# Output projection, operand sums and down projection of a retention/ConvFFN step: weights reused between column ranges, sums in place, loads spread

## The chip, the cores and the metric

The kernel runs on one core of a Trainium2 chip. The metric is the device time of one execution in microseconds (us), as the median of the runs shown. Engines are called TensorE (PE, its weight loads PEld), VectorE (DVE), ScalarE (ACT), GpSimd (POOL) and SyncE (SP, which here only issues DMAs).

## The reference

One layer, 1024 prompt frames and 64 sample frames of width 1024, all in float32. The part that the change touches:

```python
def _layer(x, c, pos0, r0, s0, conv0, ...):
    ...
    mix = jnp.concatenate([o_r, o_g], axis=-1).astype(dt)
    x = x + g1 * jnp.einsum('bte,ed->btd', mix, w_out)

    h2 = _rmsnorm(x, g_norm_ffn) * (1.0 + sc2) + sh2
    a, up = jnp.split(jnp.einsum('btd,df->btf', h2, w_ffn_in), 2, axis=-1)
    buf = jnp.concatenate([conv0.astype(a.dtype), a], axis=1)
    conv = conv_b + conv_w[0] * buf[:, 0:T]
    for j in range(1, CONV_W):
        conv = conv + conv_w[j] * buf[:, j:j + T]
    y = jax.nn.silu(conv) * up
    x = x + g2 * jnp.einsum('btf,fd->btd', y, w_ffn_out)
    return x, r_new.astype(r0.dtype), s_new.astype(s0.dtype), buf[:, T:]
```

Before it stand a first norm, an input projection and two recurrent mixers (retention and gated linear attention), behind it a last norm. D_FF is 2816, the convolution has width 3.

## The kernel before

Every float32 matmul is made of three on parts: `cut(hi, lo, src)` lets ACT round `src` into `hi`, VectorE subtracts it from `src` into `lo`, and TensorE sums hi x hi, lo x hi and hi x lo. The kernel is one long instruction order for each engine; small generators (`flow.start`, `flow.tick`) put side work between the steps of the main loops, and an engine works through its own order strictly.

**Output projection.** The 1088 columns (frames) go in three ranges, c = 0, 1, 2, of 384, 384 and 320; in each range the eight output blocks m of 128 rows run one after the other. For each step a weight unit of `w_out` (512 KB) is loaded, cut into `hi` (ACT) and `lo` (VectorE) by `take()`, multiplied into `dX` in PSUM, and freed by `release()`. The input `x`, transposed on TensorE, is added with the gain (`xt`, tile names `ab`, `hf`, `cv`), stored to `d_x2` in HBM, and its squares are summed in `sqs`. While range c runs, the second norm of range c-1 (`norm2`, scaling on VectorE, bias on ACT) is put between its steps.

**Up projection.** A Strassen-like scheme makes it of seven products of half size; `product(q, p)` multiplies weight sums by an operand `X[p]`. An operand is a cut of sums of the normed input (`operand`, `sums_b`), a weight sum is made by `need_in` and cut by `prep_in` (`prep_to` does so ahead). With the first products the norm of range 2 is finished: sums of squares by matmuls with ones, the reciprocal root `nr` on VectorE, a broadcast by matmul, then scaling.

**Down projection.** The same scheme; KF = 11 row blocks of 128. The steps run in the order M p=1 (11 steps), A p=2 (two halves u, six steps of two row blocks), A p=4 (the same), M p=6, A p=3 (u=0), M p=7, A p=3 (u=1), then p=5. For each step the weights come through `C1`, `C2` or the tile `rw` (4 buffers), `y` comes from HBM through `ry` (3 buffers) or `rb` (3 buffers, loaded from GpSimd's queue) into `ba`. `load_to` issues loads five steps ahead, `sum_out` makes weight sums three ahead, `prep_out` cuts three ahead, and `prep_b` cuts two `ba` pieces for each A step. In p=2 the sum `rw + C1` was made by VectorE, stored to HBM (`d_e`, from GpSimd's queue) and loaded again for p=3. `x3` (tile names `x_k_h`) is the residual, 16 loads of 256 KB from `d_x2`, into which `add_to` adds each finished PSUM tile (`mn`, `al`).

Of the kernel before, what the change touches and what calls it, by code (L numbers as in the profile page):

```python
# [12 lines left out]
F32 = mybir.dt.float32  # L13
# [180 lines left out]
def stream_step_kernel(  # L194
# [400 lines left out]
    for _ in range(NC3):  # L595
        for m in range(KD):
            plan(w_out[0, :, m * P:(m + 1) * P], KD, P)
# [781 lines left out]
    d_e = {}  # L1379
# [42 lines left out]
    def load_x(c, k2):  # L1422
        xt = ab_tile("ab0")[:, 0:768].rearrange("p (j d) -> p j d", j=3)
        cs = slice(k2 * 256, (k2 + 1) * 256)
# [11 lines left out]
    def operand(p, half_k, half_t, pool):  # L1436
        t = X[p] = pool.tile([P, 2, 4, HT], F32R, name=f"X{p}", bufs=1)
        for i in range(4):
            src = hf[4 * half_k + i][:, half_t * HT:half_t * HT + HT]
            cut(t[:, 0, i], t[:, 1, i], src)  # L1440
            yield 1.0

    def sums_b(which, a, b):

        for i in range(4):
            h11, h12 = hf[i][:, a:b], hf[i][:, HT + a:HT + b]
            h21, h22 = hf[4 + i][:, a:b], hf[4 + i][:, HT + a:HT + b]
            if which == 1:
                sub(h11, h12, h11)
# [7 lines left out]
    def norm2(c, sqs):  # L1457
# [11 lines left out]
        for k in range(KD):  # L1469
# [5 lines left out]
            if c < 2:  # L1475
                yield 1.2
        if c == 1:
            yield from operand(1, 0, 0, xap)
            yield from operand(2, 1, 0, xap)
# [84 lines left out]
    xr = [load_x(0, 0)]  # L1564
    for c in range(NC3):
# [4 lines left out]
        for m in range(KD):  # L1570
            (hi, lo), = take()
            ps = pair("dX")
            i = c * KD + m
            if i % 2 == 0 and i + 2 < NC3 * KD:
                xr.append(load_x((i + 2) // KD, (i + 2) % KD // 2))
            mm3(ps[:, 0, 0:w], [(hi[:, k, :], lo[:, k, :], mxs[c][k][0][:, 0:w],
                                 mxs[c][k][1][:, 0:w]) for k in (4, 5, 6, 7, 0, 1, 2, 3)])
            release()
            for j in range(3):
                tr(ps[:, 1, j * P:(j + 1) * P], xr[i // 2][:, j, (m % 2) * P:(m % 2 + 1) * P])  # L1580
# [6 lines left out]
            if m == 0:  # L1587
# [6 lines left out]
            if c == 2 and m == 5:  # L1594
# [7 lines left out]
            if c == 2 and m == 6:  # L1602
# [5 lines left out]
                                  .rearrange("j (f p) -> (j f) p", p=P))  # L1608
                prep_to(4)
                for n in range(1, 5):  # L1610
                    need_in(0, n)
# [190 lines left out]
    product(0, 1)  # L1802
    next(gen)
    turn_vectors()
# [6 lines left out]
    sums_b(1, edge, HT)  # L1811
# [128 lines left out]
    def load_out(n):  # L1940
        st = osteps[n]
        kind, p = st[:2]
        if kind == "M":
# [3 lines left out]
            elif p == 7:  # L1947
                rw[n] = ld_w(wrow(i, 0, 512, 512))
            t = ry[n] = ft("ry")
            nc.sync.dma_start(out=t, in_=d_y[i][:, YI[p]])  # L1950
        elif kind == "A":
            u, i, k = st[2:]
            if p == 2:
# [4 lines left out]
            elif p == 3:  # L1958
                t = rw[n] = ft("rw", (P, 2, 256))
                nc.sync.dma_start(out=t[:, 0:k], in_=d_e[u, i])  # L1960
# [6 lines left out]
    def sum_out(n):  # L1967
        st = osteps[n]
        kind, p = st[:2]
        if kind == "M" and p == 6:  # L1970
            w = rw[n] = ft("rw")
            sub(w, C2[:, st[2]], C1[:, st[2]])
# [379 lines left out]
```

## Time and profile before

| | |
|---|---|
| median of 3 runs | 1502.03 us (1501.88 to 1509.65) |
| profiled execution | 1507.18 us, span 1505.4 us |
| mean granted TensorE clock | 0.972 |
| busy, share of the span | PE 91%, DVE 72%, ACT 42%, POOL 21% |
| DMA | 164.31 MB, mean 109 GB/s |

The span is that of the profiled execution, on the chip's own clock from first to last instruction; its own time is 1.8 us longer. A share of busy time is a mean over stages: mixers up to about 618 us, output projection from there to about 734 us, up projection to about 1219 us, down projection to about 1490 us, and the last norm.

### The profile page before, as it was taken

What the parts mean: (1) busy time and instruction counts of PE and PEld (TensorE: products, weight loads), DVE (VectorE), ACT (ScalarE), POOL (GpSimd) and SP (SyncE); (2) the same over time, 40 slices, a digit from 0 to 9 for tenths busy, and PEclk for the clock granted to TensorE, in tenths of its full rate; (3) what the DMA queues carried; (4) which work ended last, traced back from release to release, by engine and by line L of the source; (5) the groups of instructions that cost most, each with busy time, mean ns of one, the idle gap of its engine ahead of it and who ended that gap; (6) DMA issues with size and microseconds to landing.
All of it is one profiled execution on the core that took longest, in us unless ns stands there. A gap on an engine that the chain in (4) does not pass through costs nothing.

```text
span 1505.4 us, 23828 instructions
## 1 busy us (share of the span) xinstructions
PE 1374.1 (91%) x9082; PEld 1275.0 (85%) x9082; DVE 1088.3 (72%) x2006; ACT 631.0 (42%) x1275; POOL 309.2 (21%) x416
## 2 busy tenths in 40 slices
PE   5899888989989998899779999999999998799996
PEld 3778777879979988898779999999999986688875
DVE  6647878966885788766887777777777755668775
ACT  5635434432333223555554344444444333334343
POOL 3335424414342432411000000000000011200010
PEclk9999999999999999999789999999999999899998
DMA  8420102123223223365113233222332269654522
GB/s 256 153 73 15 43 17 74 43 84 100 88 73 101 86 62 94 123 191 180 48 42 106 78 106 106 77 69 95 106 106 91 92 209 312 203 166 137 175 83 103
DMA packets 159226, 164.31 MB, mean 109 GB/s; under 512 B 9770, under 2 KB 127880, under 8 KB 159112
## 3 DMA queue, kind: packets, MB, share of 16 engines
q1 hardware_dynamic: 147655, 123.73, 26.6%
q0 software_dynamic: 11456, 39.07, 7.5%
q8 instruction: 71, 1.16, 0.3%
q14 instruction: 44, 0.35, 0.1%
HBM read 129.95 MB, written 32.81 MB: 108 GB/s over the span
## 4 chain that ended last, share of the span: by engine, by line
PE 57%; DVE 23%; issue 6%; ACT 5%; DMA 4%; POOL 1%; SPq 0%; DVEq 0%; ACTq 0%; POOLq 0%
PE dX L234 25%; PE mm L234 10%; PE dA L234 8%; PE al L234 4%; PE mn L234 3%; PE o L234 3%; DVE qbd L91 2%; DVE lo L91 2%; DVE att L91 2%; DVE acc L91 2%; ACT hi L91 1%; DVE X L91 1%; DMA rb<-d_y 1%; DVE ab L91 1%; PE sc L234 1%
## 5 line engine op out<-in xcount | busy, mean ns | idle before, releaser
L234 PE MATMUL dX<-X,lo 128*128 128x272 f32 x1344 | 182.1, 292 | 5.4 <-DVE ab L91 3.4
L234 PEld LDWEIGHTS dX<-X,lo 128*128 128x128 f32 x1344 | 175.8, 191 | 6.5 <-ACT cv L91 3.0
L234 PE MATMUL dX<-X,hi 128*128 128x272 f32 x1296 | 174.8, 291 | 4.9 <-DVE ab L91 2.7
L234 PEld LDWEIGHTS dX<-X,hi 128*128 128x128 f32 x1296 | 168.7, 191 | 5.7 <-issue 2.9
L234 PE MATMUL mm<-act_hi,hi 128*128 128x384 f32 (+1 forms) x480 | 170.1, 354 | 0.3 <-DVE mix L91 0.2
L234 PE MATMUL mm<-act_lo,hi 128*128 128x384 f32 (+1 forms) x480 | 158.1, 329 | 0.1
L234 PE MATMUL mm<-act_hi,lo 128*128 128x384 f32 (+1 forms) x480 | 157.8, 329 | 0.0
L91 ACT CAST hi<-raw 128x512 fp32r<-128x512 f32 (+1 forms) x122 | 97.3, 799 | 77.4 <-DVE raw L91 65.9
L234 PE MATMUL al<-ba,hi 128*128 128x512 f32 x396 | 102.7, 402 | 9.0 <-DVE x L91 9.0
L234 PE MATMUL mn<-lo,hi 128*128 128x512 f32 x396 | 96.5, 398 | 7.8 <-ACT lo L91 6.1
L234 PEld LDWEIGHTS mn<-lo,hi 128*128 128x128 f32 x396 | 74.3, 190 | 27.6 <-ACT lo L91 8.6
L234 PEld LDWEIGHTS al<-ba,hi 128*128 128x128 f32 x396 | 72.6, 192 | 24.4 <-DVE x L91 10.3
L234 PEld LDWEIGHTS mm<-act_hi,hi 128*128 128x128 f32 x480 | 91.5, 191 | 1.9 <-DVE mix L91 0.5
L234 PEld LDWEIGHTS mm<-act_lo,hi 128*128 128x128 f32 x480 | 91.3, 190 | 0.8 <-POOL act_lo L91 0.3
L91 DVE SCALAR_TENSOR_TENSOR cv<-ab,cw,cv 128x1088 f32<-128x1088 f32 x44 | 59.2, 1347 | 43.7 <-ACT cv L91 43.7
L234 PEld LDWEIGHTS mm<-act_hi,lo 128*128 128x128 f32 x480 | 90.8, 189 | 0.0
L234 PE MATMUL mm<-hi,act_hi 128*128 128x256 f32 x288 | 88.6, 308 | 0.2 <-ACT hi L91 0.2
L234 PE MATMUL mm<-lo,act_hi 128*128 128x256 f32 x288 | 82.8, 288 | 2.9 <-DVE lo L91 2.9
L234 PE MATMUL mm<-hi,act_lo 128*128 128x256 f32 x288 | 82.3, 286 | 0.0
L91 POOL TENSOR_TENSOR acc<-acc,prod 128x512 f32<-128x512 f32 x42 | 64.4, 1534 | 82.1 <-ACT prod L91 81.3
L234 PE MATMUL dX<-act_hi,hi 128*128 128x384 f32 (+1 forms) x192 | 67.1, 350 | 7.9 <-DVE ab L91 4.0
L91 DVE TENSOR_TENSOR lo<-raw,hi 128x1024 fp32r<-128x1024 f32 x49 | 63.7, 1302 | 13.6 <-ACT hi L91 13.5
(348 smaller groups left out, 3124.7 us busy)
## 6 DMA issues: line engine op xcount, KB each, us to landing
raw<-in_w_ffn_in_dram SPq DMA_DIRECT2D x44, 512.0 KB, 3.8
raw<-in_w_ada_dram SPq DMA_DIRECT2D x32, 512.0 KB, 4.0
raw<-in_w_in_dram SPq DMA_DIRECT2D x28, 512.0 KB, 3.8
raw<-in_w_out_dram SPq DMA_DIRECT2D x24, 512.0 KB, 3.7
d_y<-cv POOLq DMA_DIRECT2D x22, 512.0 KB, 5.1
rb<-d_y POOLq DMA_DIRECT2D x44, 256.0 KB, 3.7
rw<-in_w_ffn_out_dram SPq DMA_DIRECT2D x41, 256.0 KB, 2.7
wa<-in_w_ada_dram SPq DMA_DIRECT2D x16, 512.0 KB, 4.9
```

What stands on the lines that cost most here:

```text
L91: return call(*args, **kw)
L234: T.matmul(out, lhsT, rhs, start=start, stop=stop, skip_group_check=more)
```

## The change

- The weight units of `w_out` run in an order that turns from range to range (`M_ORDER`). The last three units of a range are not released and serve the first three steps of the next: 18 units instead of 24 are loaded and cut.
- `x` is loaded in 24 pieces of 128 columns, into tiles of its own (`xr`), instead of 12 of 256.
- The operands `X1` and `X2` are cut by column ranges, 384 columns behind the norm of range 0 and 160 behind that of range 1, instead of 544 columns behind the norm of range 1.
- The last four subtractions of `sums_b(1, ...)` run on GpSimd within the norm of range 2. The first weight sums are spread over the last steps, and `product(0, 1)` is made in two halves around the sum of the squares.
- In the down projection `C1` is overwritten by `C2 - C1` in p=6, and p=7 and p=3 load their weights again and subtract `C1`. The sums `rw + C1`, the tile `d_e`, its twelve stores and its loads are gone.
- The loads of `x3`, `x3s` and `gbc`, before at steps 2 to 6, are spread over the steps by `X3_AT`, and the loads of the first three blocks of `C1` move from step 1 to steps 12 to 14.
- `finish` has one more `yield`.

```diff
@@ -594,4 +594,6 @@
         pcol(c0)
-    for _ in range(NC3):
-        for m in range(KD):
+
+    M_ORDER = ((0, 1, 2, 3, 4, 5, 6, 7), (5, 6, 7, 4, 3, 2, 1, 0), (2, 1, 0, 3, 4, 5, 6, 7))
+    for c in range(NC3):
+        for m in M_ORDER[c][3 if c else 0:]:
             plan(w_out[0, :, m * P:(m + 1) * P], KD, P)
@@ -1378,3 +1380,2 @@
     d_y = [scr.tile([P, 7, 512], F32, name=f"d_y{i}") for i in range(KF)]
-    d_e = {}
     YI = {1: 0, 7: 1, 2: 2, 3: 3, 5: 4, 6: 5, 4: 6}
@@ -1421,5 +1422,7 @@
 
-    def load_x(c, k2):
-        xt = ab_tile("ab0")[:, 0:768].rearrange("p (j d) -> p j d", j=3)
-        cs = slice(k2 * 256, (k2 + 1) * 256)
+    def load_x(n):
+        c, m = divmod(n, KD)
+        m = M_ORDER[c][m]
+        xt = wo.tile([P, 3, P], F32, tag="xr", name="xr", bufs=4)
+        cs = slice(m * P, (m + 1) * P)
         nb = 3 if c < 2 else 2
@@ -1435,10 +1438,12 @@
 
-    def operand(p, half_k, half_t, pool):
-        t = X[p] = pool.tile([P, 2, 4, HT], F32R, name=f"X{p}", bufs=1)
+    def operand(p, half_k, half_t, pool, a=0, b=HT):
+        if p not in X:
+            X[p] = pool.tile([P, 2, 4, HT], F32R, name=f"X{p}", bufs=1)
+        t = X[p]
         for i in range(4):
-            src = hf[4 * half_k + i][:, half_t * HT:half_t * HT + HT]
-            cut(t[:, 0, i], t[:, 1, i], src)
-            yield 1.0
+            src = hf[4 * half_k + i][:, half_t * HT + a:half_t * HT + b]
+            cut(t[:, 0, i, a:b], t[:, 1, i, a:b], src)
+            yield 0.8
 
-    def sums_b(which, a, b):
+    def sums_b(which, a, b, eng=None):
 
@@ -1448,3 +1453,3 @@
             if which == 1:
-                sub(h11, h12, h11)
+                (eng or V).tensor_tensor(out=h11, in0=h12, in1=h11, op=ALU.subtract)
             elif which == 3:
@@ -1475,6 +1480,9 @@
             if c < 2:
-                yield 1.2
+                yield 1.0
+            elif k == 3:
+                sums_b(1, 2 * CW - HT, HT, G)
+        if c < 2:
+            yield from operand(1, 0, 0, xap, CW * c, (CW, HT)[c])
+            yield from operand(2, 1, 0, xap, CW * c, (CW, HT)[c])
         if c == 1:
-            yield from operand(1, 0, 0, xap)
-            yield from operand(2, 1, 0, xap)
             sums_b(1, 0, 2 * CW - HT)
@@ -1563,3 +1571,3 @@
     n2 = []
-    xr = [load_x(0, 0)]
+    xr = [load_x(0), load_x(1)]
     for c in range(NC3):
@@ -1569,13 +1577,15 @@
             G.memset(sqs[:, w:CW], 0.0)
-        for m in range(KD):
-            (hi, lo), = take()
+        for n, m in enumerate(M_ORDER[c]):
+            keep = c < 2 and n > 4
+            hi, lo = take(n - 4 if keep else 1)[-1]
             ps = pair("dX")
-            i = c * KD + m
-            if i % 2 == 0 and i + 2 < NC3 * KD:
-                xr.append(load_x((i + 2) // KD, (i + 2) % KD // 2))
+            i = c * KD + n
+            if i + 2 < NC3 * KD:
+                xr.append(load_x(i + 2))
             mm3(ps[:, 0, 0:w], [(hi[:, k, :], lo[:, k, :], mxs[c][k][0][:, 0:w],
                                  mxs[c][k][1][:, 0:w]) for k in (4, 5, 6, 7, 0, 1, 2, 3)])
-            release()
+            if not keep:
+                release()
             for j in range(3):
-                tr(ps[:, 1, j * P:(j + 1) * P], xr[i // 2][:, j, (m % 2) * P:(m % 2 + 1) * P])
+                tr(ps[:, 1, j * P:(j + 1) * P], xr[i][:, j, :])
             xt = hf[m][:, c * CW:c * CW + w]
@@ -1586,3 +1596,3 @@
             nc.gpsimd.dma_start(out=d_x2[:, m, c * CW:c * CW + w], in_=xt)
-            if m == 0:
+            if n == 0:
                 S.activation(out=sqs[:, 0:w], in_=xt, func=AF.Square)
@@ -1593,3 +1603,3 @@
             flow.tick()
-            if c == 2 and m == 5:
+            if c == 2 and n == 4:
                 do_lows(True)
@@ -1601,3 +1611,2 @@
                 raw_loads()
-            if c == 2 and m == 6:
                 ct = ab_tile("ab0")
@@ -1608,5 +1617,7 @@
                                   .rearrange("j (f p) -> (j f) p", p=P))
+            if c == 2 and n == 5:
+                prep_to(2)
+                need_in(0, 3)
+            if c == 2 and n == 6:
                 prep_to(4)
-                for n in range(1, 5):
-                    need_in(0, n)
         if c < 2:
@@ -1801,4 +1812,7 @@
     gen = norm2(2, sqs)
-    product(0, 1)
+    need_in(0, 2)
+    need_in(0, 4)
+    product(0, 1, 0, 2)
     next(gen)
+    product(0, 1, 2, 4)
     turn_vectors()
@@ -1810,3 +1824,2 @@
     product(1, 1)
-    sums_b(1, edge, HT)
     all_of(operand(5, 0, 0, xbp))
@@ -1947,3 +1960,3 @@
             elif p == 7:
-                rw[n] = ld_w(wrow(i, 0, 512, 512))
+                rw[n] = ld_w(wrow(i, 1, 512, 512))
             t = ry[n] = ft("ry")
@@ -1952,3 +1965,3 @@
             u, i, k = st[2:]
-            if p == 2:
+            if p in (2, 3):
                 rw[n] = ld_w(wpair(i, k, 1, u * 256), k)
@@ -1957,5 +1970,2 @@
                          ld_w(wpair(i, k, 0, 512 + u * 256), k))
-            elif p == 3:
-                t = rw[n] = ft("rw", (P, 2, 256))
-                nc.sync.dma_start(out=t[:, 0:k], in_=d_e[u, i])
 
@@ -1970,6 +1980,5 @@
         if kind == "M" and p == 6:
-            w = rw[n] = ft("rw")
-            sub(w, C2[:, st[2]], C1[:, st[2]])
+            sub(C1[:, st[2]], C2[:, st[2]], C1[:, st[2]])
         elif kind == "M" and p == 7:
-            sub(rw[n], C1[:, st[2]], rw[n])
+            sub(rw[n], rw[n], C1[:, st[2]])
         elif kind == "A" and p == 3:
@@ -1977,5 +1986,3 @@
             w = rw[n][:, 0:k]
-            sub(w, w, C2[:, i:i + k, u * 256:u * 256 + 256])
-
-    stores = []
+            sub(w, w, C1[:, i:i + k, u * 256:u * 256 + 256])
 
@@ -1987,3 +1994,3 @@
             c, y = main_slots(n)
-            w = C1[:, i] if p == 1 else rw.pop(n)
+            w = rw.pop(n) if p == 7 else C1[:, i]
             cut(c[:, 0], c[:, 1], w)
@@ -2006,6 +2013,2 @@
                 plus(C2[:, i:i + k, cs], v[:, 0:k], w)
-            if p == 2:
-                plus(w, w, C1[:, i:i + k, cs])
-                d = d_e[u, i] = scr.tile([P, k, 256], F32, name=f"d_e{u}_{i}")
-                stores.append((d, w))
         else:
@@ -2070,2 +2073,3 @@
             nc.sync.dma_start(out=dst_of(j), in_=yt[0:w])
+        yield 1.0
 
@@ -2127,4 +2131,9 @@
 
+
+    X3_AT = {6: [(0, 0)], 7: [(1, 0)], 8: [(2, 0)], 9: [(3, 0)]}
+    for j in range(4):
+        X3_AT[KF + 7 + j] = [(4 + j, 0)]
+        X3_AT[KF + 15 + 2 * j] = [(j, 1)]
+        X3_AT[2 * KF + 14 + 2 * j] = [(4 + j, 1)]
     altt, srs, sb = {}, [], None
-    late_stores = []
     tsq = fw.tile([P, 4, 2], F32, name="tsq", bufs=1)
@@ -2157,11 +2166,11 @@
         if n == 1:
-            for i in range(3):
-                nc.sync.dma_start(out=C1[:, i], in_=wrow(i, 0, 0, 512))
             flow.start(caches(), 1.0)
-        if n in (2, 3, 4, 5):
-            for k in (2 * n - 4, 2 * n - 3):
-                for h_ in range(2):
-                    nc.sync.dma_start(out=x3[k][h_], in_=d_x2[:, k, h_ * 512:h_ * 512 + 512])
-        if n == 6:
+        for k, h_ in X3_AT.get(n, ()):
+            nc.sync.dma_start(out=x3[k][h_], in_=d_x2[:, k, h_ * 512:h_ * 512 + 512])
+        if KF < n <= KF + 3:
+            i = n - KF - 1
+            nc.sync.dma_start(out=C1[:, i], in_=wrow(i, 0, 0, 512))
+        if n == KF + 12:
             nc.sync.dma_start(out=x3s, in_=d_x2[:, :, SEQ:T2])
+        if n == KF + 26:
             nc.sync.dma_start(out=gbc, in_=g_final[None, :].to_broadcast([P, D]))
@@ -2175,6 +2184,2 @@
             sum_out(n + 3)
-        for d, w in late_stores:
-            nc.gpsimd.dma_start(out=d, in_=w)
-        late_stores[:] = stores
-        stores[:] = []
         load_to(n + 5)
```

How the orders stand, at three places. SP, which issues DMAs in this order, at the beginning of the down projection (`C` is `C1`, `cs` a cache output, line numbers are of each kernel's own source). Before:

```order
L2159 DMA C_12852<-in_w_ffn_out_dram 128x512 x3
L1946 DMA C_12852<-in_w_ffn_out_dram 128x512
L1950 DMA ry<-d_y_6459 128x512
L2125 DMA out_dram<-cs 44x128
L2164 DMA x_0_0_12854<-d_x_6453 128x512
L2164 DMA x_0_1_12855<-d_x_6453 128x512
L2164 DMA x_1_0_12856<-d_x_6453 128x512
L2164 DMA x_1_1_12857<-d_x_6453 128x512
L1946 DMA C_12852<-in_w_ffn_out_dram 128x512
L1950 DMA ry<-d_y_6460 128x512
L2125 DMA out_dram<-cs 44x128
L2164 DMA x_2_0_12858<-d_x_6453 128x512
```

and now, from the same step's loads on:

```order
L1959 DMA C_12864<-in_w_ffn_out_dram 128x512
L1963 DMA ry<-d_y_6460 128x512
L2129 DMA out_dram<-cs 44x128
L1959 DMA C_12864<-in_w_ffn_out_dram 128x512
L1963 DMA ry<-d_y_6461 128x512
L1959 DMA C_12864<-in_w_ffn_out_dram 128x512
L1963 DMA ry<-d_y_6462 128x512
L1959 DMA C_12864<-in_w_ffn_out_dram 128x512
L1963 DMA ry<-d_y_6463 128x512
L2169 DMA x_0_0_12866<-d_x_6453 128x512
L1959 DMA C_12864<-in_w_ffn_out_dram 128x512
L1963 DMA ry<-d_y_6464 128x512
```

The loads of `C` and `ry` stand behind one another; the three early loads of `C` and the groups of four `x` loads are gone from between them.

VectorE in the last range of the output projection, from the second step on (`X_7439` and `X_7496` are `X1` and `X2`, as are `X_7020` and `X_7068` after). Before:

```order
L91 TENSOR_TENSOR sqs<-sqs,sq 128x320
L91 TENSOR_TENSOR lo<-raw,hi 128x1024
L91 SCALAR_TENSOR_TENSOR cv<-cv,A_127,dA 128x384
L91 TENSOR_TENSOR X_7439<-ab,X_7439 128x544 x2
L91 SCALAR_TENSOR_TENSOR hf<-dX,G_129,hf 128x256
L91 SCALAR_TENSOR_TENSOR hf<-dX,G_129,hf 128x64
L91 TENSOR_TENSOR sqs<-sqs,sq 128x320
L91 TENSOR_TENSOR lo<-raw,hi 128x1024
L91 TENSOR_TENSOR X_7439<-ab,X_7439 128x544
L91 TENSOR_TENSOR X_7439<-hf,X_7439 128x544
L91 TENSOR_TENSOR X_7496<-hf,X_7496 128x544
L91 SCALAR_TENSOR_TENSOR hf<-dX,G_129,hf 128x256
```

and now:

```order
L91 TENSOR_TENSOR sqs<-sqs,sq 128x320
L91 TENSOR_TENSOR X_7020<-ab,X_7020 128x160
L91 TENSOR_TENSOR lo<-raw,hi 128x1024
L91 TENSOR_TENSOR X_7020<-ab,X_7020 128x160 x2
L91 TENSOR_TENSOR X_7020<-hf,X_7020 128x160
L91 SCALAR_TENSOR_TENSOR hf<-dX,G_129,hf 128x256
L91 SCALAR_TENSOR_TENSOR hf<-dX,G_129,hf 128x64
L91 TENSOR_TENSOR sqs<-sqs,sq 128x320
L91 TENSOR_TENSOR X_7068<-hf,X_7068 128x160
L91 TENSOR_TENSOR lo<-raw,hi 128x1024
L91 TENSOR_TENSOR X_7068<-hf,X_7068 128x160
L91 TENSOR_TENSOR X_7068<-cv,X_7068 128x160 x2
```

The `X` subtractions are 160 columns wide instead of 544 and stand at the same steps, one step earlier by their last ones.

GpSimd's queue in p=2 and p=4 of the down projection. Before:

```order
L2177 DMA d_e_0_13313<-rw 128x512
L2177 DMA d_e_2_13337<-rw 128x512
L2177 DMA d_e_4_13355<-rw 128x512
L2019 DMA rb<-d_y_6456 128x512
L2019 DMA rb<-d_y_6457 128x512
L2177 DMA d_e_6_13381<-rw 128x512
L2019 DMA rb<-d_y_6458 128x512
L2019 DMA rb<-d_y_6459 128x512
L2177 DMA d_e_8_13415<-rw 128x512
L2019 DMA rb<-d_y_6460 128x512
L2019 DMA rb<-d_y_6461 128x512
L2177 DMA d_e_10_13451<-rw 128x256
```

and now:

```order
L2022 DMA rb<-d_y_6463 128x512
L2022 DMA rb<-d_y_6464 128x512
L2022 DMA rb<-d_y_6454 128x512
L2022 DMA rb<-d_y_6455 128x512
L2022 DMA rb<-d_y_6456 128x512
L2022 DMA rb<-d_y_6457 128x512
L2022 DMA rb<-d_y_6458 128x512
```

The stores `d_e` are gone, and the loads `rb` follow one another.

## Rows read from the trace of the kernel before

**Rows 1.** Windows of core 0: engine busy us, PEclk, DMA share, GB/s.

```profile
core 0: us, PE busy (x) PEld busy (x) DVE busy (x) ACT busy (x) POOL busy (x), PEclk, DMA share, GB/s
...
690.00:735.00 45.00, 34.19 (x224) 32.85 (x222) 33.09 (x72) 21.86 (x40) 5.08 (x11) 0.93 0.37 116
735.00:780.00 45.00, 34.66 (x203) 32.65 (x203) 40.05 (x89) 25.51 (x53) 1.96 (x5) 0.80 0.08 24
...
1300.00:1320.00 20.00, 11.98 (x47) 9.50 (x46) 11.20 (x18) 7.97 (x15) 4.35 (x8) 0.74 0.68 226
```

**Rows 2.** List of waits, 690 to 785 us: total, times, longest.

```profile
PE dX L234 <- DVE sqs L91: 6.6, 1, 6.6
```

**Rows 3.** Chain that ended last, 690 to 760 us: start, us, what.

```profile
737.01 3.08 PE dA L234 x12
740.10 1.29 PE dX L234 x6
```

**Rows 4.** VectorE's groups by form, 690 to 785 us: busy, mean ns.

```profile
L91 DVE TENSOR_TENSOR X<-hf,X 128x544 fp32r<-128x544 f32 x11 | 7.5, 717 | 0.0
```

**Rows 5.** VectorE's timeline in range c=1: start, us, instruction, idle before.

```profile
662.97 1.13 DVE L91 SCALAR_TENSOR_TENSOR hf<-hf,A,dA 128x384 f32<-128x384 f32 x2
...
668.49 1.13 DVE L91 SCALAR_TENSOR_TENSOR cv<-cv,A,dA 128x384 f32<-128x384 f32 x2
...
683.58 1.23 DVE L91 TENSOR_TENSOR lo<-raw,hi 128x1024 fp32r<-128x1024 f32 x1 [0.38 <-ACT hi L91]
...
688.08 1.23 DVE L91 TENSOR_TENSOR lo<-raw,hi 128x1024 fp32r<-128x1024 f32 x1 [0.38 <-ACT hi L91]
```

**Rows 6.** Chain that ended last, end of p=2 and start of p=4.

```profile
1279.33 1.40 PE al L234 x6
1280.97 1.40 PE al L234 x6
...
1293.98 4.56 DMA rb<-d_y
1298.57 0.63 ACT ba L91
1299.22 0.70 DVE ba L91
1300.75 4.85 DMA d_e<-rw
1305.65 3.19 DMA rw<-in_w_ffn_out_dram
...
1315.83 2.56 PE al L234 x6
```

**Rows 7.** GpSimd's timeline in the mixers, 318 to 326 us.

```profile
319.98 1.45 POOL L91 TENSOR_TENSOR mix<-mix,gt 128x384 f32<-128x384 f32 x1 [11.90 <-DVE gt L91]
324.18 1.01 POOL L91 TENSOR_TENSOR mix<-mix,gt 128x384 f32<-128x384 f32 x1 [2.76 <-DVE gr L91]
```

**Rows 8.** TensorE's timeline in p=1 of the down projection.

```profile
1222.81 2.89 PE L234 MATMUL mn<-lo,hi 128*128 128x512 f32 x12
...
1229.35 3.01 PE L234 MATMUL mn<-lo,hi 128*128 128x512 f32 x12
...
1235.00 0.50 PE L234 MATMUL mn<-lo,hi 128*128 128x512 f32 x1 [2.17 <-ACT lo L91]
...
1240.72 2.94 PE L234 MATMUL mn<-lo,hi 128*128 128x512 f32 x12
...
1267.75 0.63 PE L234 MATMUL al<-ba,hi 128*128 128x512 f32 x2
```

**Rows 9.** List of waits, 1215 to 1275 us, ScalarE for loads.

```profile
ACT hi L91 <- DMA C<-in_w_ffn_out_dram: 18.2, 5, 6.8
```

**Rows 10.** List of waits, 1290 to 1330 us, TensorE.

```profile
PE al L234 <- DVE x L91: 8.0, 1, 8.0
```

**Rows 11.** VectorE's timeline beside the second instruction of rows 7.

```profile
324.22 1.00 DVE L91 SCALAR_TENSOR_TENSOR ga<-ms,gr 128x6 f32<-128x6 f32 x1
...
326.68 0.16 DVE L91 SCALAR_TENSOR_TENSOR ga<-ms,gr 128x6 f32<-128x6 f32 x1
```

## The prediction

> **What bounds the kernel now.** I read the table of windows first, since a share over the whole span says nothing of one stage. In the output projection's last column range TensorE is busy 34.19 us of 45.00, in the start of the up projection 34.66 of 45.00 while VectorE is busy 40.05, and where the down projection passes from its step p=2 to p=4 it is busy 11.98 of 20.00 at a granted clock of 0.74 [rows 1]. Elsewhere TensorE is the bound. So the change can only win where TensorE stands idle, and every term below is a hole in TensorE's row, not a count of saved instructions.
>
> The list of waits names the first hole: TensorE waits 6.6 us, once, for `sqs` on VectorE [rows 2]. The chain of work that ended last shows what follows the sum of the squares: a half product of 12 matmuls takes 3.08 us, and the broadcast of the reciprocal norms runs at 740.10 [rows 3]; VectorE's work for the next products hangs on it. Timelines of VectorE and TensorE and the chain at the p=2/p=4 border give the rest.
>
> **(a) Output projection and the start of the up projection.** In the last range (c=2) ACT and DVE hand work to and fro, and `sqs` is late because eight `X` cuts and eight weight operations stand between the evictions. Removed there: eight subtractions of 128x544 at 717 ns [rows 4], 5.7 us. Added: eight of 128x160; no row has them, so 0.717 x 160/544 = 0.21 from below and 0.4 with a fixed part from above, I take 0.3, 2.4 us. Two of eight 128x512 weight operations move behind the last `sqs`; each is bounded by the 717 ns of a larger one, about 1.4 us for both. That is 4.7 us less for VectorE. The ACT copies for the same cuts shrink too and stand in the same hand-over; taking them like VectorE's at half weight adds 2.4, so `sqs` comes 7.1 us earlier. Bounds: 4.7 with VectorE alone; 10.8 if c=2 became TensorE-bound (45.00 - 34.19 [rows 1]). Now the second half of `product(0, 1)` stands between the sums of squares and the broadcast. Before, all of it ran inside the wait. The same count of 12 matmuls took 3.08 us there [rows 3]; at a clock that has not fallen it is about half. I take 2.8, since this is the same stretch with its low clock. So the broadcast comes 7.1 - 2.8 = 4.3 us earlier, and with it the VectorE-bound work behind it. Bounds 1.6 to 9.3.
>
> The cut pieces of 384 columns go into the middle range (c=1). There VectorE's dense intervals are 668.49 - 662.97 = 5.52 us, the sparse ones 688.08 - 683.58 = 4.50 [rows 5], which is TensorE's pace, since VectorE waits there. Eight cuts of about 0.717 x 384/544 = 0.51 come in, three weight subtractions of 1.23 us [rows 5] go out: almost the same sum (4.1 against 3.7), but five intervals become dense instead of sparse. Five times 1.02 is 5.1 us of lag; before, the three dense intervals lost TensorE almost nothing, so about 3 x 1.02 of lag fits into the PSUM tiles, and I charge half of the remaining 2.0: +1.0 (0 to +3).
>
> The spread of `x` in 24 pieces and the six weight units less are costed at nothing: the transfers lie under TensorE's work of 4.50 us per step. If that cover failed, each late piece would add at most one landing, 4.56 us by the longest load in [rows 6].
>
> The four 128x320 subtractions that move to GpSimd save VectorE about 4 x 0.42 = 1.7 us (0.717 x 320/544). But the `X` cuts behind them need their results, and on GpSimd a two-input operation of 128x384 took 1.01 to 1.45 us [rows 7], so the results are ready at about the same time; I take 0.1. Sum of (a): -4.3 + 1.0 - 0.1 = **-3.4** (-8 to 0).
>
> **(b) Down projection, step p=1.** Two steps at full pace take (1229.35 - 1222.81)/2 = 3.27 us each. The six from 1240.72 to 1267.75 take 27.03, against 6 x 3.27 = 19.6 [rows 8]. The waits list says why: ACT waits 18.2 us in 5 waits for the loads of `C` [rows 9], which queue on SP behind three early `C` loads and 16 `x` loads, four per step. In the changed order one or no `x` load stands between. So the excess, **-7.4**, goes (-4 if transfers of GpSimd's queue still fill the DMA engines; -9 if the wait at 1235.00, of 2.17, shrinks too). I keep that wait: it comes ahead of most `x` loads, and the `rb` loads and the cuts into `ba`, which stand behind the last `d_y` stores on GpSimd's queue, are unchanged.
>
> **(c) From p=2 to p=4.** TensorE waits 8.0 us, once, for `x` on VectorE [rows 10]. The chain before it: `rb` 4.56, ACT 0.63 and DVE 0.70 for `ba`, the store `d_e` 4.85, then the load of `rw` into the slot it frees, 3.19 [rows 6]. Without the stores the slot is free as soon as VectorE has cut the weights, and the store's 4.85 and GpSimd's waits for the sums go. What is late next is the ring of three `rb` buffers: 4.56 + 0.63 + 0.70 = 5.89 per three pieces, 1.96 each, while TensorE takes 1280.97 - 1279.33 = 1.64 per piece. Over the nine pieces of the half that can be fetched ahead, the lag grows to about 9 x 0.32 = 2.9. So the wait falls from 8.0 to about 2.9, -5.1, and with a shorter hole the clock of 0.74 [rows 1] should fall for less long: an estimate of -1.1. Sum **-6.2**. Bounds: -2 if the ring of `rb` is slower than this; -9.2 if the whole wait goes and the low clock with it: six matmuls behind it took 2.56 us, where six took 1.40 before [rows 6], 1.2 us too much.
>
> The twelve adds of 128x512 that leave VectorE and the subtractions in place cost nothing and give nothing more: VectorE is not the bound in p=2. The loads of `C`, moved to steps 12 to 14, have the whole of p=2 and p=4 before p=6 reads them. The late second group of the final norm: 0.
>
> **Sum.** -3.4 - 7.4 - 6.2 = -17.0. The profiled execution took 1507.18, so 1490.2; that is 0.34% over the median of 1502.03, so by ratio (0.9887) **1485**. About 0.5%, 7.5 us, is what a measurement of this kernel can tell from no change.
>
> **A rule weighed.** At 324.18 GpSimd runs a two-input `mix` for 1.01 us; VectorE's `ga<-ms,gr` of 128x6 beside it takes 1.00 us [rows 7, 11], the same instruction 0.16 us at 326.68. VectorE was held up for all of GpSimd's instruction. This bears on the moved sums: four GpSimd instructions next to VectorE's cuts. By the Trainium skill, "SBUF — State Buffer", section "SBUF: two separate sides", the port pair shared by the two is an exclusive lock, held for a whole instruction, against a VectorE operation with two SBUF inputs; the trace agrees.
>
> **Rivals.**
> 1. *The lock in the up projection's start.* VectorE is busy 40.05 of 45.00 there [rows 1]. If all four sums hold it up, 4 x 1.01 to 4 x 1.45 [rows 7], mean 4.9, less the 1.7 saved, (a) shrinks to -0.2: total -13.8, **1488**. Against: VectorE's scaled copies beside them read one input from PSUM. Chance 0.12.
> 2. *The `rb` ring keeps the border.* If `ba` pieces, not `rw`, were the true last release, (c) is -2: total -12.8, **1489**. For: `rb` 4.56 stands at the head of that chain. Against: TensorE was released by `x`, which stands behind the cut of `rw` on VectorE. Chance 0.14.
> 3. *More than the sum.* (a) -6, (b) -9, (c) -9.2: -24.2, **1478**. For: shorter holes leave less low clock behind them. Chance 0.14.
> 4. *Slower: late `x` loads.* The 12 `x` loads after the first four now stand on SP between `rw` loads, and SP is in order: an `rw` load that waits for a slot holds the `x` load behind it, and the add into `x` on VectorE then holds all cuts behind it. Price: one landing (4.56) for each load that comes late at its add, 12 x 4.56 = 55, so **1540** at worst; it outweighs -17.0 from the fourth on. Against: `x_4_0` is issued ten p=2 steps (2 x 1.64 each, 33 us) before its add. Chance 0.05.
> 5. *The reused weights do nothing*, (a) = 0 since c=1 gets as slow as c=2 gets fast: -13.6, **1488**. Chance 0.04.
>
> **Chances.** The sum as worked out, 1480 to 1487: 0.44. Rivals 1, 2 and 5 end at 1488 to 1489; two together would be -9 or so, 1493. Within 0.5%: two of these, or one with half of (b) gone, and rival 4 at two or three loads, 0.07 in all; slower by over 0.5%: rival 4 in full, 0.05; faster: the rest, 0.88. The range reaches to rival 3 below and to two rivals together above: 1474 to 1494.
>
> **What the profile after would show.** (a) The wait for `sqs` under 2 us, the broadcast about 4 us sooner after the projection's first matmul; wrong, if waits for weights or `x` pieces appear in c=1. (b) No waits for `C` in p=1 and steps of 3.27. (c) At the border a wait of about 3 us, released through `ba`; a wait above 6 would be rival 2. VectorE's cuts stretched beside GpSimd's sums would be rival 1, `x` loads landing after their adds rival 4. The prediction is wrong if the holes go and others of the same size open before 1219 us.

## The result, and the profile after

The changed kernel takes 1494.16 us, the median of 9 runs (1488.59 to 1496.77), against 1502.03 for the 9 of the kernel before beside it. The ratio is 0.9927 with an interval of 0.9904 to 0.9950, a gain of 11 us (8 to 14) where 17 was forecast. The profiled execution took 1496.77 with a span of 1495.0, 10.4 shorter. The side was right, and the range held by the ratio (0.9927 x 1502.03 = 1491); the median of these runs lies 0.2 us above its upper end.

The time that a kernel needs up to the output projection, whose instructions the change does not touch, came out 7.7 us apart over the profiled executions below. So I compare stretches between marks of TensorE: the projection's first matmul (604.52 before, 605.55 after; the 618 us named ahead is where its first long wait ends), the matmul on `sqs`, the broadcast of the norms, the first matmuls of p=1 and p=2, the matmul behind the wait at the border to p=4 (the fourth of p=4; three run ahead of the wait), and the last turn (transposition) of `x` (1491.62 and 1481.38). "p=4" in the table is that matmul.

| from ... to | before | forecast | after |
|---|---|---|---|
| first matmul to `sqs` | 129.63 | -6.1 | 130.22 |
| `sqs` to the broadcast | 5.75 | +2.8 | 8.60 |
| broadcast to p=1 | 479.65 | -0.1 | 479.54 |
| p=1 to p=2 | 48.20 | -7.4 | 40.34 |
| p=2 to p=4 | 45.58 | -5.1 | 41.19 |
| p=4 to the last turn | 178.29 | -1.1 | 175.94 |
| sum | 887.10 | -17.0 | 875.83 |

Where several runs have the same instructions in a stretch, their single executions differ too: the first row lies between 129.3 and 130.2 us in six of them, p=2 to p=4 between 41.2 and 41.8, and the last row between 175.0 and 176.7. So differences under 1 us in these rows, or under 2 in the last, show nothing by themselves.

The forecast is 5.7 us too large in sum. The first row alone misses by 6.7; the other rows give 1.0 of it back. TensorE's timeline after, at the projection's start (start, us, instruction, idle before):

```profile
605.55 0.44 PE L234 MATMUL dX<-act_hi,hi 128*128 128x384 f32 x1 [0.83 <-ACT gate L91]
...
619.01 0.90 PE L239 MATMUL dX<-ident,xr 128*128 128x128 f32 x3 [9.03 <-DMA xr<-in_x_prompt_dram]
```

That is nine microseconds of waiting for the first piece of `x`. The waits of SP from 595 to 640 us (total, times, longest), its timeline, and the chain that ended last in the same place say where it was:

```profile
SPq L1429 <- POOL act_lo L91: 21.2, 1, 21.2
```

```profile
616.27 1.43 SPq L1429 DMA_DIRECT2D xr<-in_x_prompt_dram  x3
```

```profile
611.81 4.44 POOL act_lo L91 x4
616.27 2.69 DMA xr<-in_x_prompt_dram
```

SP stood 21.2 us before its first load of `x`, until GpSimd's last `act_lo` of the mixers ended, and issued it at 616.27. In the kernel before, the same load went out at 594.12 (SP's timeline):

```profile
594.12 0.92 SPq L1426 DMA_DIRECT2D ab<-in_x_prompt_dram  x2
```

The tiles `xr` are in the pool `wo`, which is laid over memory that the mixers use.

The windows after, beside [rows 1]:

```profile
core 0: us, PE busy (x) PEld busy (x) DVE busy (x) ACT busy (x) POOL busy (x), PEclk, DMA share, GB/s
...
690.00:735.00 45.00, 38.60 (x264) 37.33 (x262) 30.53 (x74) 21.00 (x45) 6.68 (x18) 0.98 0.44 132
735.00:780.00 45.00, 36.22 (x204) 34.34 (x205) 36.77 (x77) 23.91 (x51) 6.00 (x11) 0.76 0.10 28
...
1300.00:1320.00 20.00, 15.70 (x74) 12.70 (x73) 12.40 (x21) 7.72 (x15) 2.73 (x5) 0.83 0.64 196
```

The last range of the projection is denser (38.60 against 34.19), the border from p=2 to p=4 too (15.70 against 11.98). The chain around the norm of range 2, beside [rows 3]:

```profile
735.77 1.44 PE dX L234 x6
737.21 2.93 PE dA L234 x12
740.13 0.42 PE dX L239 x2
...
741.48 3.09 PE dA L234 x12
744.57 1.29 PE dX L234 x6
```

Two half products of 12 matmuls stand between the sum of the squares and the broadcast, where there was one. (TensorE's timeline, from which the marks are taken, has the first matmul of the broadcast at 744.37.) TensorE still waits 4.9 us for `sqs` just before them:

```profile
PE dX L234 <- DVE sqs L91: 4.9, 1, 4.9
```

TensorE's timeline in p=1, beside [rows 8]:

```profile
1239.32 0.50 PE L234 MATMUL mn<-lo,hi 128*128 128x512 f32 x1 [2.13 <-ACT lo L91]
1240.39 4.04 PE L234 MATMUL mn<-lo,hi 128*128 128x512 f32 x11 [0.57 <-DVE lo L91]
...
1245.06 2.91 PE L234 MATMUL mn<-lo,hi 128*128 128x512 f32 x12
...
1248.28 2.89 PE L234 MATMUL mn<-lo,hi 128*128 128x512 f32 x12
...
1264.25 1.55 PE L234 MATMUL al<-ba,hi 128*128 128x512 f32 x6
```

The six steps from 1245.06 to 1264.25 take 19.19 us, 3.20 each and none with a wait, where they took 27.03; the wait at the fifth step is as it was. ScalarE still waits 3.4 us for `C`, in two waits, but nothing of it reaches TensorE. And the chain at the border, beside [rows 6]:

```profile
1287.95 5.06 DMA rb<-d_y
1293.05 1.61 issue
1294.67 3.84 DMA rb<-d_y
1298.56 1.61 issue
1300.18 3.18 DMA rb<-d_y
1303.38 0.63 ACT ba L91
...
1304.64 0.75 DVE x L91
...
1305.44 1.65 PE al L234 x3
```

Three `rb` loads one behind the other now lead to TensorE, through VectorE's add of the finished tile into `x`, and nothing of `rw`. In the list of waits the 8.0 of [rows 10] is 4.8 in two waits, of which 4.3 is the border.

### The profile page after: what moved, and what is told of

Read it like the earlier page. It is cut to its first block, busy times and chain, and to the rows that moved or that the text cites. A ratio compares the mean times of both kernels' runs of the same rounds, so it can differ in the third digit from the quotient of the medians.

```text
span 1495.0 us, 23802 instructions
## 1 busy us (share of the span) xinstructions
PE 1372.2 (92%) x9082; PEld 1277.3 (85%) x9082; DVE 1070.9 (72%) x1992; ACT 625.8 (42%) x1277; POOL 307.2 (21%) x412
## 4 chain that ended last, share of the span: by engine, by line
PE 56%; DVE 22%; issue 8%; ACT 6%; DMA 2%; POOL 1%; DVEq 0%; ACTq 0%; POOLq 0%
PE dX L234 23%; PE mm L234 10%; PE dA L234 8%; PE mn L234 5%; PE al L234 3%; PE o L234 2%; DVE lo L91 2%; DVE qbd L91 2%; DMA rb<-d_y 2%; DVE acc L91 2%; DVE att L91 1%; ACT hi L91 1%; DVE X L91 1%; PE sc L234 1%; DVE ab L91 1%
## 5 line engine op out<-in xcount | busy, mean ns | idle before, releaser
L91 ACT CAST hi<-raw 128x512 fp32r<-128x512 f32 (+1 forms) x116 | 91.1, 787 | 78.9 <-DVE raw L91 66.7
L234 PE MATMUL dA<-X,hi 128*128 128x272 f32 x552 | 74.3, 291 | 0.0
L234 PEld LDWEIGHTS dA<-X,hi 128*128 128x128 f32 x552 | 71.8, 191 | 0.0
```

What stands on the lines that cost most here:

```text
L91: return call(*args, **kw)
L234: T.matmul(out, lhsT, rhs, start=start, stop=stop, skip_group_check=more)
```

## The experiments

**x early.** Pieces of `x` in tiles that are free before the mixers end ("..." marks lines of an edit that are left out, here and below):

```diff
+    xab = [None]
...
-        xt = wo.tile([P, 3, P], F32, tag="xr", name="xr", bufs=4)
+        if n % 2 == 0:
+            xab[0] = ab_tile("ab0")
+        o = (n % 2) * 3 * P
+        xt = xab[0][:, o:o + 3 * P].rearrange("p (j d) -> p j d", j=3)
...
+            if c == 2 and n == 6:
```

The last line moves the load of the convolution's weights, which takes a tile of the same kind, two steps later.

> The changed kernel, but the 24 pieces of x go two by two into the halves of the tiles ab0, which are free before the mixers end, instead of tiles xr of the pool wo. Theory (the first x piece is issued only at 616.27, since its memory is still read by GpSimd's act_lo until then): issue near 594, no wait of 9.0 for x, the later steps of the output projection 4.8 us earlier, total -4.8 against the changed kernel. Rival (VectorE, busy with act_lo until 616.9, would hold TensorE anyway, as the 4.0 us wait of the kernel before shows): a wait for ab of 4 us or more takes its place and the gain is under 1 us beyond that.

1488.45 us, ratio to the kernel before 0.9888 (0.9861 to 0.9914). SP's timeline and TensorE's:

```profile
593.44 1.45 SPq L1434 DMA_DIRECT2D ab<-in_x_prompt_dram  x3
```

```profile
608.20 0.49 PE L239 MATMUL dX<-ident,ab 128*128 128x128 f32 x3
...
617.22 0.69 PE L234 MATMUL dX<-act_hi,hi 128*128 128x384 f32 x1 [3.96 <-DVE ab L91]
```

The load goes out 22.8 us earlier, and the old wait of 4.0 for VectorE is back, as the rival says. But from the first matmul to `sqs` it takes 125.49 instead of 130.22: -4.73, what the theory gave. The pieces' size was no part of it: they are 128 columns wide here too. By the whole time neither this edit nor either of the next two is clear of the changed kernel (0.9904 to 0.9950); the stretches are, and so is the run with all three.

**product(0, 1) whole**, ahead of the norm:

```diff
-    product(0, 1, 0, 2)
+    product(0, 1)
     next(gen)
-    product(0, 1, 2, 4)
```

> The changed kernel, but product(0, 1) runs whole before the sums of the squares, as in the kernel before. Theory (12 matmuls of 2.9 us lie between the sums and the broadcast of the norms, and the work behind hangs on the broadcast): from the end of sqs to the broadcast 6.1 us instead of 8.9, the up projection's eighth product and all behind it 2.8 us earlier, total -2.8. Rival (VectorE is the bound there and has a hole of another kind): the broadcast comes earlier, but the product at 784.74 not.

1490.66 us, 0.9906 (0.9875 to 0.9937). `sqs` to the broadcast takes 5.12 instead of 8.60, and broadcast to p=1 479.61, as before: the work behind moved with the broadcast, -3.5 (the stretch is 8.3 to 8.6 in the other runs with the half product). In the run with all three edits it is 5.78, -2.8.

**Four rb tiles:**

```diff
-    ftag = {"rw": 4, "ry": 3, "rb": 3}
+    ftag = {"rw": 4, "ry": 3, "rb": 4}
...
-        while b_load[0] < min(len(b_order), n + 3):
+        while b_load[0] < min(len(b_order), n + 4):
...
```

> The changed kernel with four rb tiles instead of three, loads issued one further ahead (one junk tile less makes room). Theory (the ring of rb of 5.9 us per three pieces is what is late at the border from p=2 to p=4): a ring of four gives 1.5 us per piece, under TensorE's 1.64, and the wait of 4.3 us falls under 1, with it the low clock; total -3.5 to -5. Rival (the pairs of weights rw and the sum C are late, two loads and five VectorE operations per step of p=4): the wait stays at 3 to 4 us.

1490.01 us, 0.9897 (0.9866 to 0.9928). TensorE's timeline at the border:

```profile
1303.56 0.97 PE L234 MATMUL al<-ba,hi 128*128 128x512 f32 x3 [1.57 <-DVE x L91]
```

The wait is 1.57, more than the 1 expected, but not the 3 to 4 of the rival; p=2 to p=4 takes 38.39 instead of 41.19. What is left comes from VectorE's own work, so the rival is right in part: its timeline has no idle time from 1300.35 to the add into `x` that releases TensorE.

```profile
1300.95 0.68 DVE L91 TENSOR_TENSOR C<-rw 128x512 f32<-128x512 f32 x1
1301.56 1.28 DVE L91 TENSOR_TENSOR ba<-rb,ba 128x512 fp32r<-128x512 f32 x2
1302.76 1.40 DVE L91 SCALAR_TENSOR_TENSOR x<-al,G,x 128x512 f32<-128x512 f32 x2
```

The three matmuls behind the wait took 0.97, not 1.65: the granted clock in the 4.5 us behind it is 1.00 (the level of 2.4 GHz), where it is 0.51 (near 1.2 GHz) in the changed kernel. Behind the border another 4.0 go (171.95 instead of 175.94; 3.0 to 4.7 against the other runs): 2.0 in the first half of p=4, where the low clock was, and a wait of 1.79 at 1447.30, which also came behind `rb`. The ring was late in both places.

**All three:**

> The changed kernel with all three: x in the tiles ab0, product(0, 1) whole, four rb tiles. If the three holes are separate, the gains add: 4.8 + 2.8 + 4 = 11.6 us under the changed kernel, 23 under the kernel before. If one of them only hides another (VectorE in the projection's start, the wait at p=3), the sum comes out at 7 or less.

1479.51 us, 0.9830 (0.9805 to 0.9855); 14.65 under the changed kernel by the medians, 14.4 between first matmul and last turn. The gains add: 4.8, 2.8, and 2.8 and 3.2 on either side of the border; the other 0.9 lies in the two stretches between, within what single executions differ by.

**The x3 burst back:**

```diff
...
+    X3_AT = {n: [(k, h_) for k in (2 * n - 4, 2 * n - 3) for h_ in range(2)] for n in (2, 3, 4, 5)}
...
         if n == 1:
+            for i in range(3):
+                nc.sync.dma_start(out=C1[:, i], in_=wrow(i, 0, 0, 512))
...
```

> The changed kernel with the 16 loads of x3 back at steps 2 to 5, four per step, and the three early loads of C1 back at step 1; x3s and gbc stay late. Theory (the loads of C waited behind this burst): the waits of ScalarE for C come back, p=1 of the down projection lasts 48.2 us instead of 40.3, total +7.9, about 1502. Rival (the gain in p=1 came from GpSimd's queue or from gbc and x3s): p=1 stays near 40 to 43 us.

1498.37 us, 0.9974 (0.9955 to 0.9994), 0.47% over the changed kernel's ratio, 7 us. Its profiled execution is no use, since the whole program took 4624.57 us in it, with TensorE busy for 4594.2. So the same kernel ran once more:

> The same kernel as in the run with the x3 burst, for a profile in which TensorE runs at its usual pace. Theory: from the first matmul of p=1 to the first of p=2 48.2 us instead of 40.3, with ScalarE waiting for C in five steps. Rival (SP's other loads moved, not the burst): 40 to 43 us.

1495.69 us. p=1 to p=2 takes 47.14 instead of 40.34, +6.8; from first matmul to last turn it is +4.7, since 0.9 comes back at the border and the rest lies in stretches that the edit doesn't touch. A row of TensorE's timeline, and of the list of waits from 1215 to 1275 us:

```profile
1242.54 0.50 PE L234 MATMUL mn<-lo,hi 128*128 128x512 f32 x1 [1.47 <-ACT lo L91]
```

```profile
ACT hi L91 <- DMA C<-in_w_ffn_out_dram: 8.7, 3, 2.9
```

ScalarE waits for `C` again, in three steps and not five, so `x3s` and `gbc`, which stay late here, may have had a part in the last ones. The burst with the three `C1` loads is nearly all of the 7.86 us, and since the next run has the three loads back without the burst and keeps 40.34, it is the burst itself.

**The store back:**

```diff
...
+            if p == 2:
+                plus(w, w, C1[:, i:i + k, cs])
+                d = d_e[u, i] = scr.tile([P, k, 256], F32, name=f"d_e{u}_{i}")
+                stores.append((d, w))
...
+        for d, w in late_stores:
+            nc.gpsimd.dma_start(out=d, in_=w)
...
```

> The changed kernel with the sums rw + C1 made in p=2, stored to d_e and loaded again for p=3, as before; since p=2 then reads C1 from its first step, the three early loads of C1 stand at step 1 again. Theory (store and slot are what made the wait at the border 8.0 us): the first matmul of p=4 comes 45.6 us behind the first of p=2 instead of 41.2, total +4.4 to +6 with the low clock, and SP waits for the stores. Rival (the ring of rb alone sets it, as the run with four rb tiles suggests): under +1.5. The three loads of C1 may cost up to 2 us in p=1.

1498.45 us, 0.9971 (0.9950 to 0.9992). TensorE's timeline at the border, and the waits of SP from 1219 to 1330 us:

```profile
1309.94 1.65 PE L234 MATMUL al<-ba,hi 128*128 128x512 f32 x3 [7.90 <-DVE x L91]
```

```profile
SPq L1944 <- DMA d_e<-rw: 40.3, 11, 8.4
```

p=2 to p=4 takes 46.87, +5.68; p=1 to p=2 40.34, so the three early `C1` loads alone cost nothing. With the store, the store is late; without it, the ring is. Both theories hold, one behind the other.

**Sums on VectorE:**

```diff
-                sums_b(1, 2 * CW - HT, HT, G)
+                sums_b(1, 2 * CW - HT, HT)
```

> The changed kernel with the last four subtractions of sums_b(1) on VectorE, at the same place in the norm of range 2. Theory: the work from the broadcast of the norms to the last VectorE-bound product lasts 40.2 us on either engine, total within 0.5. Rival 1 (the shared port: GpSimd's sums hold VectorE up): it gets shorter by 1 us or more. Rival 2 (GpSimd takes load off VectorE): it gets longer by about 1.7.

1493.20 us in one run. From the broadcast to p=1 480.12 against 479.54, half a microsecond above what the other runs spread (478.24 to 479.65); from first matmul to last turn 876.11 against 875.83. Up to the last product bound by VectorE it is 1.3 longer, as rival 2 has it, but most of that is not left at p=1. No hold-up of VectorE by GpSimd shows.

**Cuts whole**, behind the norm of range 1:

```diff
-            yield from operand(1, 0, 0, xap, CW * c, (CW, HT)[c])
-            yield from operand(2, 1, 0, xap, CW * c, (CW, HT)[c])
+            pass
         if c == 1:
+            yield from operand(1, 0, 0, xap)
+            yield from operand(2, 1, 0, xap)
```

> The changed kernel with X1 and X2 cut in one piece of 544 columns behind the norm of range 1, as before. Theory: the middle range loses its lag of 2.6 us, and the last range gets eight cuts of 544 instead of 160 columns, +3.0 us on VectorE and up to +2.4 on ScalarE: from the projection's first matmul to the sum of the squares 130.2 us becomes 130.6 to 133. Rival (the cuts lie under TensorE's work in the last range anyway): it falls to 127.6.

1492.75 us, 0.9935 (0.9913 to 0.9956), not apart from the changed kernel. First matmul to `sqs` takes 131.90, +1.7: inside the theory's span. So cutting by ranges is worth 1.7 us there, not the 6.1 of the whole term (the table under "(a), the two ranges" below takes it apart); between first matmul and last turn (876.00) even that is lost in the spread.

**Natural order** of the weight units:

```diff
-    M_ORDER = ((0, 1, 2, 3, 4, 5, 6, 7), (5, 6, 7, 4, 3, 2, 1, 0), (2, 1, 0, 3, 4, 5, 6, 7))
+    M_ORDER = (tuple(range(KD)),) * 3
...
-            keep = c < 2 and n > 4
+            keep = False
...
-            if c == 2 and n == 4:
+            if c == 2 and n == 5:
```

> The changed kernel with the weight units of w_out in the natural order in each range, 24 loaded and cut, none kept; the forced cuts of the next weights one step later, as before. Theory (the three kept units pay for the cuts of X that moved into the middle range): three more weight cuts of 2.3 us on ScalarE and VectorE in the first steps of each of the two later ranges, from the projection's first matmul to the sum of squares 3 to 6 us more than 130.2. Rival (the weight cuts lie under TensorE's work): under +1.

1498.74 us in one run. First matmul to `sqs` takes 130.28 against 130.22; the theory falls. TensorE's timeline there still has the wait for `x` (8.9), which could hide the cuts, so the fastest kernel (all three edits and the late `ba` below) got the same edit:

> The fastest kernel (x in ab0, product(0, 1) whole, four rb tiles, late cuts into ba) with the weight units of w_out in the natural order, 24 loaded and cut. If the late x alone gave ScalarE and VectorE the slack that hid the six more weight cuts in the run with the natural order, the time from the projection's first matmul to the sum of squares grows from 125.7 us to 128 or more, since x is early here; if the cuts lie under TensorE's work, it stays under 126.5 and the total at 1476 to 1477.

1475.72 us, 0.9789 (0.9761 to 0.9817); first matmul to `sqs` takes 125.62, against 125.66 in that kernel. Six loads of 512 KB and six weight cuts on ScalarE and VectorE cost nothing that can be measured.

**Late ba:** the fifth step of p=1, ahead of which ScalarE waits for an `rb` load (list of waits of the changed kernel, 1215 to 1275 us):

```profile
ACT ba L91 <- DMA rb<-d_y: 8.9, 1, 8.9
```

The edit, on top of all three:

```diff
+            while b_load[0] < 4:
+                load_b()
             flow.start(caches(), 1.0)
...
-        if n > 0:
+        if n > 4:
             prep_b()
```

> The kernel with all three edits (x in the tiles ab0, product(0, 1) whole, four rb tiles), and the first rb loads issued at step 1 and cut into ba only from step 5 on. Theory (the wait of 2.1 + 0.6 us at the fifth step of p=1 is ScalarE's in-order cut into ba, which waits for an rb load behind the last d_y stores): both waits and the low clock behind them go, p=1 lasts 36 instead of 40.2 us, total -4 against the kernel with all three, 1475.5. Rival (the six cuts into ba that move into p=2 are late there): p=1 gets shorter, and p=2 or its border longer by the same.

1476.37 us, 0.9798 (0.9776 to 0.9820). TensorE's timeline at the first matmuls of p=1 and p=2:

```profile
1216.81 2.95 PE L234 MATMUL mn<-lo,hi 128*128 128x512 f32 x12
...
1252.30 1.55 PE L234 MATMUL al<-ba,hi 128*128 128x512 f32 x6
```

35.49 us instead of 40.19, and 38.45 instead of 38.40 to p=4: the theory, and nothing given back later. From first matmul to last turn it is 857.29, 18.5 less than in the changed kernel. This kernel and the one with the natural order are the fastest of the study, and their intervals overlap.

## Why the prediction was right, and where it was off

**(a), the cover that was not there.** The step that failed is the sentence that `x` in 24 pieces costs nothing since the transfers lie under TensorE's work. I had weighed the size of the pieces and not the memory that they go to. The cost was one hole at the first piece, whose load was issued 22 us later, and 4.73 us of it reach `sqs` (x early). This is most of the 5.7 missing. My fallback, one landing of 4.56 for each late piece, priced something else: the transfer itself took 2.69 us, and it was the issue that came late. The sign that I had named, a wait for `x` in c=1, appeared in c=0, and so did the last one, a hole before 1219 us of the size of those that went.

**(a), the two ranges.** Without that hole the stretch would have shrunk by 129.63 - 125.49 = 4.1 us instead of 6.1. TensorE's timeline, at the first matmul, the last turn of `x` in c=0 and in c=1, and `sqs`, says which of the two terms was off. Before:

```profile
604.52 0.44 PE L234 MATMUL dX<-act_hi,hi 128*128 128x384 f32 x1 [0.83 <-ACT gate L91]
...
647.11 0.49 PE L239 MATMUL dX<-ident,ab 128*128 128x128 f32 x3
...
684.90 0.49 PE L239 MATMUL dX<-ident,ab 128*128 128x128 f32 x3
...
734.15 1.41 PE L234 MATMUL dX<-ones,sqs 128*128 128x1 f32 x6 [6.63 <-DVE sqs L91]
```

and after:

```profile
652.83 0.49 PE L239 MATMUL dX<-ident,xr 128*128 128x128 f32 x3
...
693.40 0.49 PE L239 MATMUL dX<-ident,xr 128*128 128x128 f32 x3
```

The same marks in four runs:

| range | before | after | x early | cuts whole |
|---|---|---|---|---|
| first (c=0) | 42.59 | 47.28 | 42.50 | 47.26 |
| middle (c=1) | 37.79 | 40.57 | 40.64 | 38.41 |
| last (c=2), to `sqs` | 49.25 | 42.37 | 42.35 | 46.23 |

The 7.1 for the last range was right: it is 6.9. The term that was mis-sized is the lag of the middle range, +1.0 in the sum and +2.8 measured, near the bound of +3. Three of its steps grew from 4.50 us to 5.92, 5.55 and 5.10, so less of the lag was taken up by the PSUM tiles than I had allowed; no run shows why. With whole cuts the middle range gives 2.2 back and the last one loses 3.9, which is the 1.7 above. So the cuts are 3.9 of the 6.9; the other 3.0 belongs to what else left the last range, above all the weight operations, and no run separates that. What was *not* in the sum, the six weight units, is truly nothing (natural order, twice).

**(a), the half product.** +2.85 against +2.8, and the whole product takes it back: the wait of 4.9 us for `sqs` that is left has room for the other half. Two signs that I had named for (a) failed by this and by the hole: the wait for `sqs` is not under 2 us, and the broadcast comes 138.8 us behind the first matmul instead of 135.4, later and not 4 us sooner.

**(a), GpSimd's sums.** -0.1 forecast, -0.1 measured, and at most 0.6 by the run on VectorE. Rival 1, the lock, falls. GpSimd's and VectorE's timelines after:

```profile
747.24 2.55 POOL L91 TENSOR_TENSOR ab<-ab 128x320 f32<-128x320 f32 x3 [6.53 <-ACT ab L91]
749.75 0.89 POOL L91 TENSOR_TENSOR hf<-hf 128x320 f32<-128x320 f32 x1
```

```profile
747.64 1.83 DVE L91 SCALAR_TENSOR_TENSOR hf<-hf,A,dX 128x256 f32<-128x256 f32 x6
749.39 1.25 DVE L91 SCALAR_TENSOR_TENSOR cv<-cv,A,dX 128x256 f32<-128x256 f32 x4
...
752.20 2.00 DVE L91 TENSOR_TENSOR X<-ab,X 128x544 fp32r<-128x544 f32 x3 [1.55 <-ACT X L91]
```

VectorE's scaled copies, six in 1.83 us, run on beside three of GpSimd's sums in 2.55; in the kernel before, where GpSimd has nothing beside them, the six `hf` copies took 1.83 too. `X` starts behind both, on ScalarE. The copies read `dX` from PSUM. In the Trainium skill, "SBUF — State Buffer", section "SBUF: two separate sides", a VectorE operation takes the lock when it has two SBUF inputs or runs in a two-port mode; the trace agrees, here by its absence and in [rows 7, 11] by the 1.00 us.

**(b).** -7.4 forecast, -7.86 measured; the wait at the fifth step stayed, as said, and its cause was the one named (late ba). A step took 3.20 us and not 3.27.

**(c).** The mechanism was right: the store goes, the ring of `rb` is late next, and the release comes through `ba`. The term was mis-sized: a wait of 4.3 instead of 2.9, and the stretch -4.4 instead of -5.1. The two rounds of the ring in the chain after took 1294.67 - 1287.95 = 6.72 and 1300.18 - 1294.67 = 5.51 us, 6.1 in the mean and not 5.89; by the prediction's own working that gives 9 x 0.40 = 3.6. The other 0.7 may be the add into `x` behind the last `ba` (0.75), which I had not counted; no run shows that, and in five other runs with the same instructions the wait is 4.3 to 5.0. Of the -4.4, the wait is 3.7; the rest is p=2 itself, where a wait of 0.5 for an add at 1287.06 is gone. The bound of -2 was not reached, so rival 2 is half true. What lies behind p=4 gave -2.35 instead of -1.1: a wait of 1.22 for `hi` at 1481.31, which I had left out, is gone, and the first half of p=4 took 0.7 less: behind the shorter wait the granted clock is 0.52 for 4.7 us and 1.00 from 1310.1 on, where before it is 0.50 for 4.9 us and still 0.89 in the next 4.8. So (c) is -6.7 against -6.2, right in sum by two errors of opposite sign.

Rival 4, the late `x3` loads, did not come: apart from the border, no wait for `x` above 1.8 us stands in TensorE's timeline after, and the border's chain leads through `rb`, not through a load of `x`.

That the time lies in the range is in part luck. The range was made wide for rivals 1, 2 and 5, and what used it up was a hole that none of them names; (b) and the row behind p=4, 1.7 us better than forecast, made up for some of it.

## What to carry to other kernels

A buffer that moves to another pool inherits that pool's memory, and with it the end of the last stage that used it: before a load is costed at nothing, look up who still reads the place it goes to, not only what work covers the transfer. When a chain with two resources in it loses one (here the store and the slot), price the other as the new wait, and from several landings, not one. And work taken out of steps in which it does not hold TensorE up is worth nothing, here even six loads of 512 KB and a quarter of the weight cuts, while the narrower cuts in the last range, where TensorE waits for VectorE, were worth 3.9 us there.

## What was not expected

- The projection's first matmul, with unchanged arithmetic ahead of it, came between 599.73 and 607.43 us over the profiled executions, 0.5% of the whole time. Differences of a few us between single executions have to be read from stretches.
- A single execution of one program took 4624.57 us, with TensorE busy 99% of it and every other engine at its usual busy time (VectorE 1066.1 us); nine others of it took 1496.46 to 1507.10. What it was stays open.
